# Moving the large SBUF tiles to multiples of 1 KB, and swapping two first loads

## The chip, the cores and the metric

The kernel runs on one core of a Trainium2 chip. The metric is device time in microseconds, the median over runs of the same program.

## What is computed

One layer of a hybrid decoder on 256 tokens of width 2048, all in float32. Cut to what matters here:

```python
h = rmsnorm(x, ln_g)
proj = h @ w_in + b_in                      # 2048 -> 18956 columns
# mLSTM branch (6 heads), retention branch (6 heads), both causal over 256 tokens
ml_out  = head_layernorm(mlstm(silu(conv(q, k)), v, i, f)) * sigmoid(o) * silu(z)
rt_out  = head_layernorm(retention(rope(q), rope(k), v)) * silu(z)
# cross-attention (4 heads) into 256 memory tokens
mk, mv  = split(rmsnorm(mem, mem_ln_g) @ w_mem_kv)
xa_out  = softmax(xa_q @ mk.T / 16) @ mv * silu(xa_z)
merged  = g0 * (ml_out @ w_br_ml) + g1 * (rt_out @ w_br_ret) + g2 * (xa_out @ w_br_xa)
y       = rmsnorm(x + merged @ w_out, final_g)
```

## The kernel before, in words

**The products.** Every weight matrix is cut into column chunks, 512 columns wide (the last two of `w_out` 256 wide). A chunk's weights come in slabs `raw` of 128 partitions x 2048 float32, one DMA of 1 MB each on SP's queue, three buffers deep. ScalarE rounds half a slab to fp32r (`wh`, 1024 columns, four buffers) and VectorE writes the rest `raw - wh` (`wl`, four buffers). The activations are split the same way into a high and a low tile. For every block of 128 rows and every half of the tokens `products` then issues three matmuls into one PSUM bank: `wh` with the high activations, `wl` with the high ones, `wh` with the low ones. Below, these three are a **triple**. The activations are the stationary operand (`lhsT`, 128 x 128, 512 B a partition), the weights the moving one (`rhs`, 512 columns, 2 KB a partition):

```python
PE.matmul(ps, lhsT=h, rhs=a, start=kt == 0, stop=False)          # L924: wh, high
PE.matmul(ps, lhsT=h, rhs=b, start=False, stop=False)            # L925: wl, high
PE.matmul(ps, lhsT=l, rhs=a, start=False, stop=kt == nk - 1)     # L926: wh, low
```

**Where the stationary operand lies.** Four pairs of buffers serve as high and low activations, one pair at a time: `mgd` and `oT1` for the memory tokens (`w_mem_kv`); `aTh` and `aTl` for x (`w_in`); parts of `oT1` and `oT2` for a branch's output (`w_br_*`); and `aTh` and `aTl` once more for the merged branches (`w_out`). The buffer number is left out in the profile, so `oT1` and `oT2` read as `oT`. While the memory tokens are in work, the slot of `aTl` holds their raw form (`memraw`).

**Order of the work.** All instructions are recorded in the order in which they are to stand (a manual schedule). `split` runs three half slabs ahead of `products`; between two half slabs one step of a background job (attention, mLSTM and retention cores, convolution, rotary, transposes) is put in. TensorE is one stream of both.

**Addresses.** The pool gives every tag its place in a partition in the order in which `til` first names it, at the next multiple of 32 B, behind 1 KB that is reserved. Small tiles therefore shift everything that is named after them.

**The start.** ScalarE's queue issues the first piece of memory tokens (`memraw[:, 0, :]`, 128 KB) and then `memG`, the norm weights of the memory tokens (8 KB); SP's queue issues the first slab's pieces and the other memory tokens. The first work of ScalarE, `split_act` (L269), multiplies the one by the other and so needs both.

Of the kernel before, what the change touches and what calls it, by code (L numbers as in the profile page):

```python
# [9 lines left out]
F32R = mybir.dt.float32r  # L10
I32 = mybir.dt.int32
# [5 lines left out]
P = 128  # L17
D = 2048
T = 256
NKT = D // P  # L20
NML = 6
# [7 lines left out]
CST_W = NKT + 48 + 12 * 3 + 1 + 64 + P + P  # L29
# [121 lines left out]
def body(ctx, tc, A, out):  # L151
    nc = tc.nc
    V, S, G, PE = nc.vector, nc.scalar, nc.gpsimd, nc.tensor
# [6 lines left out]
    def til(tag, shape, dt=F32, bufs=1):  # L160
        names[tag] = names.get(tag, 0) + 1
        return sb.tile(shape, dt, tag=tag, name=f"{tag}_{names[tag]}", bufs=bufs)

    def bank(tag="bg", bufs=4):
        names[tag] = names.get(tag, 0) + 1
        return pp.tile([P, 512], F32, tag=tag, name=f"{tag}_{names[tag]}", bufs=bufs)
# [4 lines left out]
    def f32(ap):  # L171
        return ap.bitcast(F32)
# [19 lines left out]
    n = _ROWS["w_mem_kv"] // 512  # L192
# [3 lines left out]
    halves = {}  # L196


    memG = til("memG", [P, NKT])
    memraw = til("aTl", [P, NKT, T])  # L200
    S.dma_start(memraw[:, 0, :], A["memT"][:, 0, :])
    S.dma_start(memG, A["mem_ln_g"])
    ones = til("ones", [P, P])
    G.memset(ones, 1.0)
    nhalf = til("nhalf", [P, 4])
    G.memset(nhalf, -0.5)
    S.copy(til("warm", [P, 1]), ones[:, 0:1])
    wps = bank()
    for _ in range(NWARM):
        PE.matmul(wps[:, :P], lhsT=ones, rhs=ones, start=True, stop=True)  # L210
# [36 lines left out]
    for si in range(NRAW):  # L247
        dma(si)

    cst = til("cst", [P, CST_W])  # L250
    off = [0]

    def part(w):
        off[0] += w
        return cst[:, off[0] - w:off[0]]
# [1 line left out]
    xG, convw, convb = part(NKT), part(48).rearrange("p (b k) -> p b k", k=4), part(12)  # L257
    hg = {"ml_hnorm_g": part(12), "ret_hnorm_g": part(12)}
    bif, freq, ident, mask = part(1), part(64), part(P), part(P)
    posi = til("posi", [P, 2], I32)  # L260
    dret = [None]

    aTh = til("aTh", [P, NKT, T], F32R)
    aTl = til("aTl", [P, NKT, T], F32R)
    ssq = {n: til("ss_" + n, [P, 2]) for n in ("mem", "x")}
    rms = {n: til("r_" + n, [P, 2]) for n in ("mem", "x")}

    def split_act(h, l, src, g):
        S.activation(h, src, AF.Copy, bias=0.0, scale=g)  # L269
# [57 lines left out]
                split_act(aTh[:, kt, :], aTl[:, kt, :], raw[:, k * T:(k + 1) * T], xG[:, kt:kt + 1])  # L327


    cosT = til("cosT", [P, 2, 64])  # L330
    sinT = til("sinT", [P, 2, 64])
    inv2pi = _inv2pi_parts()

    def trig_job():
# [46 lines left out]
        yield  # L381


    MT = til("MT", [P, T], F32R)
    sel = til("sel", [P, NML], F32R)
    cT = til("cT", [P, 2, P])
    enm = til("enm", [P, 2, NML])

    def gate_rows_job(psif):
        rows = iter(range(8))  # L390
# [41 lines left out]
        G.memset(zero, 0.0)  # L432
        G.tensor_copy(MT, zero)
        V.tensor_tensor(sel, ident[:, 0:6], ident[:, 32:38], op=ALU.add)
# [6 lines left out]
        V.scalar_tensor_tensor(RT[64:70], b, -1.0, M, op0=ALU.mult, op1=ALU.subtract)  # L441
        V.tensor_copy(MT[:6], M)
        V.tensor_tensor(MT[32:38], M, f32(MT[:6]), op=ALU.subtract)
        yield
# [161 lines left out]
    def ml_core(h):  # L606
        p, hh = divmod(h, 2)

        mb = bank()
        PE.matmul(mb[:, :T], lhsT=sel[:, h:h + 1].to_broadcast([P, P]), rhs=MT, start=True, stop=True)  # L610
        dm = til("core", [P, 512], bufs=4)
# [67 lines left out]
    gs = {}  # L679
    merged = [None]  # L680
    bigy = {}
    st_out = til("ssy", [P, 2, 5])
    sumsq = til("sumsq", [P, 2])

    def silu_into(dst, ps, bias, r, extra=None):
        zu = stage()
# [276 lines left out]
def _inv2pi_parts():  # L963

    from fractions import Fraction
    pi = Fraction(314159265358979323846264338327950288419716939937510582097494459230781640628620899,
                  10 ** 80)
    x = 1 / (2 * pi)
    parts, shift = [], 14
    for i in range(5):  # L970
        sc = 2 ** shift
        c = Fraction(int(x * sc), sc)
        parts.append(float(c))
        x -= c
        shift += 12
    return parts
# [53 lines left out]
def _build(host):  # L1030
    import concourse.bacc as bacc
    nc = bacc.Bacc("TRN2", target_bir_lowering=False, num_devices=1, dynamic_dma_scratch_size=1024)
    A, arrays = {}, {}
    for n, v in host.items():
        arrays[f"in_{n}_dram"] = v
        A[n] = nc.dram_tensor(f"in_{n}_dram", v.shape, mybir.dt.from_np(v.dtype), kind="ExternalInput").ap()
    out = nc.dram_tensor("out_0_dram", (1, T, D), F32, kind="ExternalOutput").ap()
    with tile.TileContext(nc) as tc:
        body(tc, A, out[0])
    return nc, arrays  # L1040
# [7 lines left out]
```

## Time and profile before

| | |
|---|---|
| median of 3 runs | 1222.71 us (1222.61 to 1223.24) |
| the profiled execution, its own time | 1222.62 us |
| its span in the trace | 1220.6 us |
| TensorE busy | 1211.6 us (99% of the span) |
| VectorE busy | 759.0 us (62%) |
| ScalarE busy | 585.9 us (48%) |
| TensorE's granted clock, share of full speed | 0.999 |

The span is what the trace covers; the 2.0 us between it and the execution's own time lie around it. A busy share is an average over the whole span.

### The profile page before, as it was taken

What the parts mean: (1) busy time and instruction counts of PE and PEld (TensorE: products, weight loads), DVE (VectorE), ACT (ScalarE), POOL (GpSimd) and SP (SyncE); (2) the same over time, 40 slices, a digit from 0 to 9 for tenths busy, and PEclk for the clock granted to TensorE, in tenths of its full rate; (3) what the DMA queues carried; (4) which work ended last, traced back from release to release, by engine and by line L of the source; (5) the groups of instructions that cost most, each with busy time, mean ns of one, the idle gap of its engine ahead of it and who ended that gap; (6) DMA issues with size and microseconds to landing.
All of it is one profiled execution on the core that took longest, in us unless ns stands there. A gap on an engine that the chain in (4) does not pass through costs nothing.

```text
span 1220.6 us, 14366 instructions
## 1 busy us (share of the span) xinstructions
PE 1211.6 (99%) x5490; PEld 1004.2 (82%) x5490; DVE 759.0 (62%) x994; ACT 585.9 (48%) x705; POOL 143.0 (12%) x164
## 2 busy tenths in 40 slices
PE   9999999999999999999999999999999999999997
PEld 7888888888888888888888888888888888888887
DVE  6564576565557576776775555657767665567554
ACT  6665454445434554554555443344444444444443
POOL 0006404400000130130120102101010000000001
PEclk9999999999999999999999999999999999999999
DMA  9876656565556547657547555575657665567752
GB/s 370 317 288 237 238 194 214 200 212 188 205 206 233 200 173 262 215 178 274 202 171 281 194 193 201 196 250 173 237 211 242 232 217 214 186 240 257 290 187 90
DMA packets 61413, 270.65 MB, mean 222 GB/s; under 512 B 7072, under 2 KB 22304, under 8 KB 33312
## 3 DMA queue, kind: packets, MB, share of 16 engines
q1 hardware_dynamic: 56592, 258.06, 59.7%
q10 hardware_dynamic: 4752, 11.68, 2.6%
q8 instruction: 43, 0.70, 0.2%
q14 instruction: 26, 0.21, 0.0%
HBM read 256.60 MB, written 13.11 MB: 221 GB/s over the span
## 4 chain that ended last, share of the span: by engine, by line
PE 98%; DMA 0%; issue 0%; DVE 0%; SPq 0%; ACT 0%; POOLq 0%; POOL 0%; DVEq 0%; ACTq 0%
PE d L925 32%; PE d L924 32%; PE d L926 31%; PE bg L517 1%; PE bg L492 1%; DMA raw<-in_w_dram 0%; PE bg L602 0%; PE bg L604 0%; PE bg L603 0%; PE bg L664 0%; PE bg L622 0%; PE bg L880 0%; PE bg L879 0%; PE bg L508 0%; PE bg L665 0%
## 5 line engine op out<-in xcount | busy, mean ns | idle before, releaser
L274 DVE TENSOR_TENSOR wl<-raw,wh 128x1024 fp32r<-128x1024 f32 (+1 forms) x432 | 528.1, 1229 | 385.9 <-ACT wh L273 385.3
L273 ACT CAST wh<-raw 128x1024 fp32r<-128x1024 f32 (+1 forms) x432 | 443.6, 1033 | 477.4 <-PE d L926 421.7
L924 PE MATMUL d<-wh,aTh 128*128 128x512 f32 (+1 forms) x1344 | 522.4, 389 | 0.0
L925 PE MATMUL d<-wl,aTh 128*128 128x512 f32 (+1 forms) x1344 | 521.3, 388 | 0.0
L926 PE MATMUL d<-wh,aTl 128*128 128x512 f32 (+1 forms) x1344 | 516.8, 385 | 0.0
L924 PEld LDWEIGHTS d<-wh,aTh 128*128 128x128 f32 x1344 | 252.4, 188 | 54.0
L926 PEld LDWEIGHTS d<-wh,aTl 128*128 128x128 f32 x1344 | 252.3, 188 | 53.1
L925 PEld LDWEIGHTS d<-wl,aTh 128*128 128x128 f32 x1344 | 252.7, 188 | 48.4
L926 PE MATMUL d<-wh,oT 128*128 128x512 f32 x384 | 149.4, 389 | 0.0
L924 PE MATMUL d<-wh,oT 128*128 128x512 f32 x256 | 99.6, 389 | 0.0
L925 PE MATMUL d<-wl,oT 128*128 128x512 f32 x256 | 99.6, 389 | 0.0
L926 PEld LDWEIGHTS d<-wh,oT 128*128 128x128 f32 x384 | 72.1, 188 | 15.0
L925 PEld LDWEIGHTS d<-wl,oT 128*128 128x128 f32 x256 | 48.1, 188 | 10.0
L924 PEld LDWEIGHTS d<-wh,oT 128*128 128x128 f32 x256 | 48.1, 188 | 10.0
L689 POOL TENSOR_TENSOR gz<-gz,st 128x512 f32<-128x512 f32 x16 | 21.5, 1357 | 259.9 <-ACT gz L688 259.9
L924 PE MATMUL d<-wh,mgd 128*128 128x512 f32 x128 | 50.1, 392 | 0.2 <-ACT wh L273 0.2
L925 PE MATMUL d<-wl,mgd 128*128 128x512 f32 x128 | 50.0, 391 | 0.3 <-DVE wl L274 0.2
L831 POOL TENSOR_TENSOR oT<-oT,oT 128x512 f32<-128x512 f32 (+1 forms) x8 | 9.2, 1159 | 214.6 <-ACT st L829 214.6
L558 POOL TENSOR_TENSOR k<-k,gs 128x1024 f32<-128x1024 f32 x3 | 7.4, 2472 | 212.7 <-ACT k L556 212.7
L459 DVE SCALAR_TENSOR_TENSOR st<-d,r_x,bias 128x512 f32<-128x512 f32 x44 | 31.4, 744 | 0.0
L924 PEld LDWEIGHTS d<-wh,mgd 128*128 128x128 f32 x128 | 24.1, 188 | 5.8 <-ACT wh L273 0.8
L925 PEld LDWEIGHTS d<-wl,mgd 128*128 128x128 f32 x128 | 24.0, 188 | 5.8 <-DVE wl L274 1.0
(192 smaller groups left out, 626.5 us busy)
## 6 DMA issues: line engine op xcount, KB each, us to landing
raw<-in_w_dram SPq DMA_DIRECT2D x209, 1024.0 KB, 4.8
bias<-in_bias_dram SPq DMA_DIRECT2D x37, 256.0 KB, 5.2
td<-tx SPq DMA_DIRECT2D x52, 128.0 KB, 2.8
ty<-td ACTq DMA_DIRECT2D x13, 512.0 KB, 5.0
td<-tx SPq DMA_DIRECT2D x64, 64.0 KB, 3.2
ty<-td ACTq DMA_DIRECT2D x16, 256.0 KB, 5.6
oT<-in_x_dram SPq DMA_DIRECT2D x3, 1024.0 KB, 7.1
raw<-in_w_dram SPq DMA_DIRECT2D x5, 512.0 KB, 6.8
```

The costliest lines, as they stand in the source:

```text
L273: S.copy(wh, raw)
L274: V.tensor_tensor(wl, raw, f32(wh), op=ALU.subtract)
L459: V.scalar_tensor_tensor(dst, ps, r, bias, op0=ALU.mult, op1=ALU.add)
L492: PE.matmul(ps[:, tb * T:(tb + 1) * T], lhsT=qT[:, 2 * hh + db, tb * P:(tb + 1) * P], rhs=kT[:, 2 * hh + db, :], start=db == 0, stop=db == 1)
L517: PE.matmul(ps[:, tb * T:(tb + 1) * T], lhsT=pT[:, c:c + P], rhs=v[:, mb, hh * T:(hh + 1) * T], start=mb == 0, stop=mb == 1)
L558: G.tensor_tensor(qf, qf, yf, op=ALU.mult)
L689: G.tensor_tensor(dst, dst, zu, op=ALU.mult)
L831: G.tensor_tensor(y, y, g[:, c0:c0 + W], op=ALU.mult)
L924: PE.matmul(ps, lhsT=h, rhs=a, start=kt == 0, stop=False)
L925: PE.matmul(ps, lhsT=h, rhs=b, start=False, stop=False)
L926: PE.matmul(ps, lhsT=l, rhs=a, start=False, stop=kt == nk - 1)
```

## The change

Two things are done. First, the small tiles (norm weights, constants, tables, sums) are all named at the top of `body`, followed by an unused tile of 256 B, `fill`; the first large tile, `aTl`, and all that follow then begin at 7168 B. No tile changes its size and no large tile its neighbours, but `aTh` no longer has the small tiles around it. The places before and now:

```
tile (B a partition)     before: address, mod 1024     now: address, mod 1024
aTl    (16384)              1216   192                    7168     0
mgd    (16384)             18176   768                   23552     0
oT1    (16384)             34560   768                   39936     0
gs     (12288)             50944   768                   56320     0
oT2    (8192)              63232   768                   68608     0
raw    (3 x 8192)          71424   768                   76800     0
aTh    (16384)             97728   448                  101376     0
wh     (4 x 4096)         117504   768                  117760     0
wl     (4 x 4096)         133888   768                  134144     0
st     (4 x 2048)         150272   768                  150528     0
k      (2 x 4096)         158464   768                  158720     0
v      (2 x 4096)         183040   768 (2nd: 800)       183296     0 (2nd: 32)
q      (4160)             195424   864                  195680    96
core   (4 x 2048)         209888   992                  210144   224
```

Second, ScalarE's queue issues `memG` first and the first piece of memory tokens after it. The core of the diff:

```diff
     memG = til("memG", [P, NKT])
+    nhalf = til("nhalf", [P, 4])
+    warm = til("warm", [P, 1])
+    ones = til("ones", [P, P])
+    cst = til("cst", [P, CST_W])
...
+    MT = til("MT", [P, T], F32R)
+    cT = til("cT", [P, 2, P])
+    til("fill", [P, 64])
     memraw = til("aTl", [P, NKT, T])
+    S.dma_start(memG, A["mem_ln_g"])
     S.dma_start(memraw[:, 0, :], A["memT"][:, 0, :])
-    S.dma_start(memG, A["mem_ln_g"])
-    ones = til("ones", [P, P])
     G.memset(ones, 1.0)
-    nhalf = til("nhalf", [P, 4])
     G.memset(nhalf, -0.5)
-    S.copy(til("warm", [P, 1]), ones[:, 0:1])
+    S.copy(warm, ones[:, 0:1])
```

On ScalarE's queue the head of the program stood so before (a name's number is the buffer's):

```order
L201 DMA aTl_66<-in_memT_dram 128x256
L202 DMA memG_65<-in_mem_ln_g_dram 128x16
L207 ACT_TABLE_LOAD
L207 COPY warm_73<-ones_69 128x1
L269 ACTIVATE mgd_86<-aTl_66,memG_65 128x256
L273 CAST wh_119<-raw_90 128x512
```

and stands so now:

```order
L217 DMA memG_65<-in_mem_ln_g_dram 128x16
L218 DMA aTl_84<-in_memT_dram 128x256
L221 ACT_TABLE_LOAD
L221 COPY warm_67<-ones_68 128x1
L279 ACTIVATE mgd_101<-aTl_84,memG_65 128x256
L283 CAST wh_120<-raw_105 128x512
```

The two loads have changed places; no other instruction of any engine has moved, which the triples of a `w_in` chunk on TensorE show for the middle of the program, before:

```order
L924 MATMUL d_29_4758<-wh_4865,aTh_105 128x512
L925 MATMUL d_29_4758<-wl_4866,aTh_105 128x512
L926 MATMUL d_29_4758<-wh_4865,aTl_106 128x512
L924 MATMUL d_29_4759<-wh_4865,aTh_105 128x512
L925 MATMUL d_29_4759<-wl_4866,aTh_105 128x512
```

and now, at the same place:

```order
L926 MATMUL d_29_4759<-wh_4866,aTh_118 128x512
L927 MATMUL d_29_4759<-wl_4867,aTh_118 128x512
L928 MATMUL d_29_4759<-wh_4866,aTl_119 128x512
L926 MATMUL d_29_4760<-wh_4866,aTh_118 128x512
L927 MATMUL d_29_4760<-wl_4867,aTh_118 128x512
```

Only the line numbers and the numbers of the buffers differ: lines of `products` are two higher, and the operands lie elsewhere.

## Rows read from the trace of the kernel before

**Rows 1.** The page: busy time, and the chain that ended last.

```profile
PE 1211.6 (99%) x5490; PEld 1004.2 (82%) x5490; DVE 759.0 (62%) x994; ACT 585.9 (48%) x705; POOL 143.0 (12%) x164
...
PE 98%; DMA 0%; issue 0%; DVE 0%; SPq 0%; ACT 0%; POOLq 0%; POOL 0%; DVEq 0%; ACTq 0%
```

**Rows 2.** Waits of TensorE: us in total, times, longest.

```profile
PE bg L210 <- POOL nhalf L206: 1.0, 1, 1.0
PE d L924 <- ACT wh L273: 0.2, 1, 0.2
PE d L925 <- DVE wl L274: 0.2, 1, 0.2
```

**Rows 3.** Groups by form, whole span: busy us, mean ns of one.

```profile
L924 PE MATMUL d<-wh,aTh 128*128 128x512 f32 x1280 | 504.5, 394 | 0.0
...
L924 PE MATMUL d<-wh,oT 128*128 128x512 f32 x256 | 99.6, 389 | 0.0
L924 PE MATMUL d<-wh,mgd 128*128 128x512 f32 x128 | 50.1, 392 | 0.2 <-ACT wh L273 0.2
...
L926 PE MATMUL d<-wh,aTl 128*128 128x256 f32 x64 | 17.9, 280 | 0.0
```

**Rows 4.** Timeline of TensorE: first and last high product of 450 to 480.

```profile
450.27 0.39 PE L924 MATMUL d<-wh,aTh 128*128 128x512 f32 x1
...
479.79 0.39 PE L924 MATMUL d<-wh,aTh 128*128 128x512 f32 x1
```

**Rows 5.** Windows of line 924 alone: length, busy (count), weight loads, clock, DMA, GB/s.

```profile
450.00:480.00 30.00, 17.06 (x44) 8.26 (x44) 1.00 0.77 270
720.00:750.00 30.00, 17.20 (x45) 8.26 (x44) 1.00 0.53 180
...
30.00:60.00 30.00, 17.12 (x44) 8.31 (x45) 1.00 0.87 320
...
141.80:150.20 8.40, 4.77 (x12) 2.24 (x12) 1.00 0.55 203
```

**Rows 6.** Timeline of TensorE: first and last high product of 720 to 750.

```profile
719.96 0.39 PE L924 MATMUL d<-wh,oT 128*128 128x512 f32 x1
...
749.88 0.39 PE L924 MATMUL d<-wh,oT 128*128 128x512 f32 x1
```

**Rows 7.** Timeline of TensorE: first and last high product of 30 to 60.

```profile
30.25 0.39 PE L924 MATMUL d<-wh,mgd 128*128 128x512 f32 x1
...
59.49 0.39 PE L924 MATMUL d<-wh,mgd 128*128 128x512 f32 x1
```

**Rows 8.** Timeline of TensorE in a `w_out` chunk.

```profile
1184.87 0.39 PE L924 MATMUL d<-wh,aTh 128*128 128x512 f32 x1
...
1186.93 0.39 PE L924 MATMUL d<-wh,aTh 128*128 128x512 f32 x1
```

**Rows 9.** Timeline of TensorE after the gate rows, to the next background matmuls.

```profile
141.89 0.40 PE L924 MATMUL d<-wh,aTh 128*128 128x512 f32 x1
...
149.59 0.40 PE L924 MATMUL d<-wh,aTh 128*128 128x512 f32 x1
...
150.29 1.89 PE L492 MATMUL bg<-k,q 128*128 128x256 f32 x8
```

**Rows 10.** Chain that ended last, to 20 us: start, us, what.

```profile
2.57 5.94 DMA raw<-in_w_dram
8.52 0.02 issue
8.54 0.63 ACT wh L273
```

**Rows 11.** Timeline of ScalarE at the start, with idle time before.

```profile
4.79 0.51 ACT L269 ACTIVATE mgd<-aTl,memG 128x256 fp32r<-128x256 f32 x1 [1.66 <-DMA memG<-in_mem_ln_g_dram]
...
8.54 0.62 ACT L273 CAST wh<-raw 128x512 fp32r<-128x512 f32 x1 [1.05 <-DMA raw<-in_w_dram]
```

**Rows 12.** DMA issues of the first 2 us: KB each, us to landing.

```profile
aTl<-in_memT_dram ACTq DMA_DIRECT2D x1, 128.0 KB, 3.6
aTl<-in_memT_dram SPq DMA_DIRECT2D x1, 128.0 KB, 3.4
memG<-in_mem_ln_g_dram ACTq DMA_DIRECT2D x1, 8.0 KB, 3.5
```

**Rows 13.** Waits of the whole span: ScalarE for TensorE.

```profile
ACT wh L273 <- PE d L926: 421.7, 277, 3.4
```

**Rows 14.** Timeline at 654 us: a split on VectorE, and the product that uses it.

```profile
654.31 1.23 DVE L274 TENSOR_TENSOR wl<-raw,wh 128x1024 fp32r<-128x1024 f32 x1 [0.20 <-ACT wh L273]
...
655.87 0.39 PE L925 MATMUL d<-wl,aTh 128*128 128x512 f32 x1
```

More of the change, by code (lines that the diff above doesn't have):

```diff
@@ L199, in body @@
     memG = til("memG", [P, NKT])
+    nhalf = til("nhalf", [P, 4])
+    warm = til("warm", [P, 1])
+    ones = til("ones", [P, P])
+    cst = til("cst", [P, CST_W])
+    posi = til("posi", [P, 2], I32)
+    ssq = {n: til("ss_" + n, [P, 2]) for n in ("mem", "x")}
+    rms = {n: til("r_" + n, [P, 2]) for n in ("mem", "x")}
+    cosT, sinT = (til(n, [P, 2, 64]) for n in ("cosT", "sinT"))
+    sel = til("sel", [P, NML], F32R)
+    enm = til("enm", [P, 2, NML])
+    st_out = til("ssy", [P, 2, 5])
+    sumsq = til("sumsq", [P, 2])
+    MT = til("MT", [P, T], F32R)
+    cT = til("cT", [P, 2, P])
+    til("fill", [P, 64])
     memraw = til("aTl", [P, NKT, T])
+    S.dma_start(memG, A["mem_ln_g"])
     S.dma_start(memraw[:, 0, :], A["memT"][:, 0, :])
-    S.dma_start(memG, A["mem_ln_g"])
-    ones = til("ones", [P, P])
     G.memset(ones, 1.0)
-    nhalf = til("nhalf", [P, 4])
     G.memset(nhalf, -0.5)
-    S.copy(til("warm", [P, 1]), ones[:, 0:1])
+    S.copy(warm, ones[:, 0:1])
     wps = bank()
@@ L248, in body @@
         dma(si)
-    cst = til("cst", [P, CST_W])
     off = [0]
@@ L259, in body @@
     bif, freq, ident, mask = part(1), part(64), part(P), part(P)
-    posi = til("posi", [P, 2], I32)
     dret = [None]
@@ L264, in body @@
     aTl = til("aTl", [P, NKT, T], F32R)
-    ssq = {n: til("ss_" + n, [P, 2]) for n in ("mem", "x")}
-    rms = {n: til("r_" + n, [P, 2]) for n in ("mem", "x")}
     def split_act(h, l, src, g):
@@ L327, in split_aux @@
                 split_act(aTh[:, kt, :], aTl[:, kt, :], raw[:, k * T:(k + 1) * T], xG[:, kt:kt + 1])
-    cosT = til("cosT", [P, 2, 64])
-    sinT = til("sinT", [P, 2, 64])
     inv2pi = _inv2pi_parts()
@@ L381, in trig_job @@
         yield
[L384 to L387, printed above, removed]
     def gate_rows_job(psif):
@@ L681, in body @@
     bigy = {}
-    st_out = til("ssy", [P, 2, 5])
-    sumsq = til("sumsq", [P, 2])
     def silu_into(dst, ps, bias, r, extra=None):
```

## The prediction

> **What bounds the kernel now.** I read the page first. TensorE is busy for 1211.6 of 1220.6 us, and the chain that ended last runs through TensorE for 98% of the span [rows 1]. The waits of TensorE confirm it: one of 1.0 us before the warm-up and two of 0.2 us near the start, nothing later [rows 2]. Behind them the other engines wait for TensorE and not the reverse: ScalarE stood 421.7 us in all until a product had freed a `wh` buffer [rows 13]. So an edit changes the time only if it changes how densely matmuls follow each other, or when their stream begins.
>
> A busy engine need not be at its best, so the next view is the spacing of the matmuls, by stationary operand. The change moves operands, and the spacing is the only thing in the trace that could feel an address. A duration in the profile spans several matmuls in the pipeline (392 or 389 ns, with starts some 228 ns apart), so I go from start to start. In an undisturbed `w_in` stretch the high product of line 924 starts at 450.27 us and the last one at 479.79 us [rows 4]; 44 of them stand there [rows 5], so 43 triples took 29.52 us: 686.5 ns each, 228.8 ns a matmul. In a branch projection, 45 starts from 719.96 to 749.88 us [rows 5, 6] give 44 triples in 29.92 us: 680.0 ns. In the memory stage, 44 starts from 30.25 to 59.49 us [rows 5, 7] give 43 triples in 29.24 us: 680.0 ns again. All three ran at a granted clock of 1.00, the 2.4 GHz level [rows 5].
>
> The three stretches do the same arithmetic with the same shapes and with the same `wh` and `wl` slots as moving operand. What differs is the stationary operand's place: 768 mod 1024 for `mgd`, `oT1` and `oT2`, which is also that of `wh` and `wl`; 448 and 192 for `aTh` and `aTl`. The stage is not the cause: in `w_out`, with other data and other background work but once more in the `aTh` and `aTl` slots, three triples take 1186.93 - 1184.87 = 2.06 us, 687 ns [rows 8]. Nor is traffic: the DMA engines were busy for a share of 0.77 in the slow stretch, but for 0.87 in the memory stage, which is at 680 [rows 5]. And `mgd` with `oT1`, two separate tiles, is as fast as `oT1` with `oT2`. I conclude that a stationary operand at 64 mod 128 (as 448 and 192 both are) costs TensorE some 6.5 ns a triple, or that one at another remainder than the moving operand does; the trace can't tell these apart.
>
> **The change, part by part.**
>
> *Large tiles to 1 KB.* The order of instructions stays, so the same 1,280 triples of 512 columns run from `aTh` and `aTl` [rows 3]. Both slots go to 0 mod 1024, and `wh` and `wl` too; their blocks lie 512 B apart, so stationary and moving operand then stand to each other as `mgd` and `wh` do now, and the remainder mod 128 is 0. Under either reading they take the 680.0 ns of the other stages: 1,280 x 6.5 ns = **8.3 us** less.
>
> Some stretches are slower than 686.5. After the gate rows twelve starts run from 141.89 to 149.59 us [rows 5, 9]: eleven triples in 7.70 us, 700 ns each. Such stretches come back a few times and are short. If they also fall to 680, this one gives another 12 x 13.5 ns = 0.16 us. The mean duration of a high product from `aTh`, 394 ns against 389 from `oT` [rows 3], also holds matmuls that queue behind background ones, and an address won't free those. I bound this term by 0 and by six stretches of the size shown, 1.0 us, and take **0.6 us**, since the memory and branch stages show a high product at the same 389 whatever runs beside them.
>
> The last two chunks have 64 triples of 256 columns [rows 3], for which no operand at another place is on record. I bound them by 0 and by the same 6.5 ns, 0.4 us, and take **0.2 us**, the middle.
>
> The triples of `mgd` and `oT` (128 and 256) [rows 3] move from 768 to 0 with `wh` and `wl` together; nothing relative changes, and I take 0. The background tiles (`k`, `q`, `v`, `core`) all move by 256 B together and stay off 1 KB where they were off it: 0. VectorE, ScalarE and the DMAs also read and write at other places, but work ahead of TensorE [rows 13], so a change there is hidden. That cover is thinnest where I found a split on VectorE ending at 655.54 us for a product that began at 655.87 us [rows 14], a lead of 0.33 us. TensorE 1% faster over the some 30 us before would use up 0.3 us of it. If that lead goes under, the wait is a few tenths of a us, at that place; I allow 0.3 us as a bound and take 0.
>
> *The two loads of ScalarE's queue.* Before, the first ACTIVATE starts at 4.79 us, when `memG` lands, having waited 1.66 us [rows 11]. It took 3.5 us to land, and a piece of memory tokens 3.6 us on the same queue and 3.4 us on SP's [rows 12]. A swap therefore exchanges which of the two lands second; the second is issued at the same time and needs 3.4 to 3.6 us in either case, so the first ACTIVATE moves by -0.1 to +0.1 us, or later if 128 KB behind the other loads take longer. But what ends last at the start is neither. The chain runs through the first slab's third piece, ordered at some 2.1 us, on its way until 8.52 us and rounded at 8.54 us [rows 10]; ScalarE stood idle for 1.05 us before that [rows 11]. So an earlier `memG` gains nothing, and tokens that come up to 1.05 us later cost nothing. Bounds: 0.3 us either way, for the slab's piece that shares the engines with the swapped load. Value: 0.
>
> **Sum.** 8.3 + 0.6 + 0.2 = 9.1 us. The profiled execution took 1222.62 us, 0.1 us under the median of 1222.71, so from the median the forecast is 1222.7 - 9.1 = **1213.6 us**. Bounds: the gain is at least 8.3 - 0.3 - 0.3 = 7.7 us and at most 8.3 + 1.0 + 0.4 + 0.3 = 10.0 us, which is 1212.7 to 1215.0.
>
> **Rivals.**
>
> *No change.* The 6.5 ns come from something that goes with `aTh` and `aTl` but not with their remainder, say from how far they lie from `wh`, which hardly changes (`aTh` still ends just below `wh`). For it: the three matmuls of a triple aren't slowed alike, which a plain alignment cost would do. Against it: the 16 blocks of `aTh` and the four buffers of `wh` lie at many distances, and 43 triples in a row show one mean. Time: 1222.7 less at most the 0.3 us of the start, 1222.4 to 1223.
>
> By the Trainium skill the address shouldn't count either. TensorE: Matmul & The Clock Gate gives TensorE two independent read ports, one for the moving and one for the stationary operand (Step-by-step: what each phase is for), and a spacing that follows from the column count alone, 512/2.4 + 2.5 = 216 ns (Back-to-back issue gap). By that page the sum would be 0. The trace doesn't agree: neither 226.7 nor 228.8 ns is 216, and the spacing depends on the slot.
>
> *Slower: a common start at 0 collides.* If reads of both operands that begin at 0 mod 1024 hamper each other more than those at 768, every triple of 512 columns could run at the 700 ns that this kernel knows [rows 9]: 1,280 x 13.5 ns + 384 x 20 ns = 25 us, 1248 us. Against it: at 768 they share a remainder already and are the fastest. It decides from the first stretch on: a spacing above 680 ns in the memory stage would say so; over 2.4 us are lost once the 1,664 triples average 1.5 ns more than now.
>
> *A larger gain.* 226.7 ns is still 13 ns above 512/2.4 = 213.3. If 0 mod 1024 is better than 768 as 768 is better than 448, by 6.5 ns on each of 1,664 triples, another 10.8 us go: 1203 us. No row shows an operand of this size at 0, so it stays a small chance.
>
> **Chances.** The forecast 0.80, no change 0.11, slower 0.04, the larger gain 0.05. What a measurement of this kernel can tell from no change is some 0.2%, 2.4 us. So: faster 0.85, same 0.11, slower 0.04. The range must hold 8 in 10 and so may leave out the rivals, but holds the forecast's own bounds with 0.6 us for the spread of runs, and at the slow end a gain that is only three quarters of the main term, as it is if one of the two slots keeps a part: 1211.5 to 1216.0 us.
>
> **What would show it.** In the trace after: triples of `aTh` at 680 ns between 450 and 480 us (or still 686.5: no change), those of `mgd` still at 680; no 700 ns stretch after the gate rows; the first continuous product still at some 10 us, behind the same piece of the slab; TensorE's waits still only at the start. I am wrong if the spacing is a matter of place and not of alignment, or if 0 isn't as good as 768.

## The result, and the profile after

The changed kernel takes 1216.19 us, the median of 6 runs (1215.39 to 1218.67), against 1222.74 us for the kernel before in 6 runs beside it: a ratio of 0.9947, 95% interval 0.9934 to 0.996. It is faster by 6.5 us, where 9.1 were forecast, and 0.2 us above the range.

The triples are where the forecast saw them. The timeline of TensorE after, at the place of [rows 4]:

```profile
450.50 0.39 PE L926 MATMUL d<-wh,aTh 128*128 128x512 f32 x1
...
479.74 0.39 PE L926 MATMUL d<-wh,aTh 128*128 128x512 f32 x1
```

29.24 us are 43 triples of 680.0 ns (the window below counts 45 products, of which one had begun at 449.82 us), where there were 686.5. The windows of the high product after, against [rows 5]:

```profile
450.00:480.00 30.00, 17.20 (x45) 8.26 (x44) 1.00 0.76 269
720.00:750.00 30.00, 17.12 (x44) 8.29 (x45) 1.00 0.55 191
30.00:60.00 30.00, 17.12 (x44) 8.32 (x45) 1.00 0.83 313
```

All three stages now hold the same number of triples but for the edges. The chain is still TensorE's, with 98%.

Two things went the other way. The first is at the end. Groups by form of the 256-column products, after (before: 280 ns, [rows 3]), and the timeline in their midst:

```profile
L928 PE MATMUL d<-wh,aTl 128*128 128x256 f32 x64 | 18.1, 283 | 0.0
```

```profile
1200.80 0.28 PE L926 MATMUL d<-wh,aTh 128*128 128x256 f32 x1
...
1202.96 0.28 PE L926 MATMUL d<-wh,aTh 128*128 128x256 f32 x1
```

Six triples in 2.16 us are 360 ns each. Before, six took 2.12 us, 353.3 ns each:

```profile
1204.15 0.28 PE L924 MATMUL d<-wh,aTh 128*128 128x256 f32 x1
...
1206.27 0.28 PE L924 MATMUL d<-wh,aTh 128*128 128x256 f32 x1
```

The second is the start, in this one execution. Windows of the first 16 us after: length, busy (count) of TensorE, its weight loads, VectorE, ScalarE, GpSimd, then granted clock, DMA share, GB/s:

```profile
0.00:4.00 4.00, 3.02 (x15) 3.02 (x16) 0.00 (x0) 1.48 (x2) 0.43 (x6) 1.00 0.50 147
4.00:8.00 4.00, 2.44 (x12) 1.74 (x11) 1.57 (x3) 1.43 (x3) 0.00 (x0) 0.91 0.92 302
8.00:12.00 4.00, 3.64 (x8) 2.11 (x7) 2.44 (x5) 3.03 (x6) 0.00 (x0) 0.50 1.01 405
12.00:16.00 4.00, 4.00 (x15) 3.18 (x14) 3.38 (x5) 2.98 (x5) 0.00 (x0) 0.74 0.96 363
```

The granted clock fell to 0.50, the 1.2 GHz level, for the stretch from 8 to 12 us and parts of its neighbours. Ahead of that TensorE had been idle: the timeline shows the last warm-up matmul ending at 4.83 us and the first product after a wait of 1.32 us, and the waits of TensorE have a row that [rows 2] lacks:

```profile
6.15 0.49 PE L926 MATMUL d<-wh,mgd 128*128 128x512 f32 x1 [1.32 <-ACT wh L283]
```

```profile
PE d L926 <- ACT wh L283: 1.7, 2, 1.3
```

The first high product from `aTh` came at 97.6 us in place of 94.2, 3.4 us late, while from there to the last one the program was 7.3 us shorter. The tile view of `aTh`, before and after (min/median/max, first and last start):

```profile
L924 PE MATMUL d<-wh,aTh x1344: 279/392/584, 94.2 to 1212.6; 128*128 128x512 f32 x183, 128*128 128x256 f32 x9
```

```profile
L926 PE MATMUL d<-wh,aTh x1344: 278/389/586, 97.6 to 1208.7; 128*128 128x512 f32 x183, 128*128 128x256 f32 x9
```

This profiled execution is the one of 1218.67 us; the other five, with a mean clock of 0.999, took 1215.39 to 1216.61.

### The profile page after: what moved, and what is told of

It reads as the page before. It is cut to its first block, busy times and chain, and to the rows that moved or that the text cites. A ratio compares the mean times of both kernels' runs of the same rounds, so it can differ in the third digit from the quotient of the medians.

```text
span 1216.7 us, 14366 instructions
## 1 busy us (share of the span) xinstructions
PE 1206.4 (99%) x5490; PEld 1005.2 (83%) x5490; DVE 759.4 (62%) x994; ACT 587.2 (48%) x705; POOL 143.0 (12%) x164
## 4 chain that ended last, share of the span: by engine, by line
PE 98%; DMA 1%; issue 0%; DVE 0%; SPq 0%; ACT 0%; POOLq 0%; POOL 0%; DVEq 0%; ACTq 0%
PE d L926 32%; PE d L927 32%; PE d L928 32%; PE bg L496 1%; PE bg L521 1%; DMA raw<-in_w_dram 1%; PE bg L606 0%; PE bg L608 0%; PE bg L607 0%; PE bg L626 0%; PE bg L668 0%; PE bg L882 0%; PE bg L881 0%; PE bg L512 0%; PE bg L627 0%
```

## The experiments

Theory A, formed after the result, had the swap of the two loads, which makes the first product later, to blame for what was missing. On the places there were two readings to tell apart, the place itself or the distance of the operands.

**New places, old order of loads.**

```diff
-    S.dma_start(memG, A["mem_ln_g"])
     S.dma_start(memraw[:, 0, :], A["memT"][:, 0, :])
+    S.dma_start(memG, A["mem_ln_g"])
```

> Theory A (the swap of the two loads costs at the start what is missing): with the large tiles at multiples of 1 KB and the old order of loads, the first product of the memory stage starts at 5.9 us again, the granted clock stays at 1.00 from there on, and the time is 1222.7 - 7.3 = 1215.4 us with a spread of runs under 1 us. Rival B (the new places of the tiles delay the start): the first product still starts at 6.1 us or later, and the runs still lie between 1215.4 and 1218.7 us, with a median of some 1216.2 us. In both, triples from aTh and aTl take 680 ns.

Measured: 1215.69 us (1215.12 to 1216.44), ratio 0.9941 (0.9928 to 0.9953); first product at 5.99 us; triples at 680 ns.

**Old places, new order of loads** (the kernel before with the two lines exchanged).

> Theory A: with the old places and the swapped loads the kernel is slower than before by 0.3 to 3.4 us, different from run to run, with a median of some 1223.5 us; the first product starts at 6.1 us or later. Rival B: 1222.7 us, first product at 5.9 us. Triples from aTh and aTl take 686.7 ns in both.

Measured: 1223.59 us in 11 runs (1222.63 to 1224.22) against 1222.93, ratio 1.0005 (0.9996 to 1.0014): no difference that can be told, though the first product came at 6.32 us. The mean clock lay between 0.997 and 0.999.

**The changed kernel with more warm-up**, `NWARM = 16` for 10.

> The changed kernel with 16 warm-up matmuls in place of 10, which fill TensorE's idle time from 4.8 us to the first product at 6.1 us. Theory A with idle TensorE as the reason for the fall of the granted clock: the clock no longer falls in any run (mean 0.999), and the median is some 1215.5 us. Rival C (the fall has nothing to do with that idle time, only with the later waits for the slab): the clock falls as often as in the changed kernel, median 1216.2 us.

Measured: 1215.61 us (1215.38 to 1215.66), the narrowest of all.

**The changed kernel once more.**

> The changed kernel once more, as a control beside the three others: 1215.4 to 1218.7 us, median 1216.2 us, with a granted clock of 0.995 in the longest runs and 0.999 in the shorter ones, if theory A is right that the loss at the start differs from run to run.

Measured: 1215.82 us (1215.56 to 1216.61), ratio 0.9943 (0.993 to 0.9955), with a mean clock of 0.998 or 0.999 in each run. Windows of its start, first product after 0.54 us of idle time:

```profile
4.00:8.00 4.00, 3.23 (x14) 2.46 (x14) 2.35 (x5) 2.35 (x5) 0.00 (x0) 1.00 0.93 318
8.00:12.00 4.00, 3.81 (x17) 2.84 (x16) 2.69 (x5) 3.28 (x5) 0.00 (x0) 1.00 1.02 416
```

So theory A falls as an account of what was missing: with the new places the swap made 0.13 us of difference (1215.82 against 1215.69 us), which the spread of the runs covers. It isn't shown that the swap is free. With the old places the median rose by 0.66 us, to where theory A had put it; the interval of the ratio still holds 1, so a few tenths of a us are neither shown nor excluded. A mean clock of 0.995, the fall, came once in 11 runs of the changed kernel and in none of the 15 with more warm-up, these and those below: too rare to say that the warm-up cures it.

The mean clock also misses shorter losses. In the trace of the old places with the new order, with a mean of 0.999, the first products stood 0.43 us apart, as in the low stretch of the trace after, where later ones stand 0.23 us apart (the windows of this trace give 1.00 there, so the level is read from the spacing alone):

```profile
8.07 0.63 PE L924 MATMUL d<-wh,mgd 128*128 128x512 f32 x1
...
9.35 0.63 PE L924 MATMUL d<-wh,mgd 128*128 128x512 f32 x1
```

There the first high product from `aTh` came at 95.4 us in place of 94.2. Of the ten traces of the layer's kernel, the three that show this spacing are the three in which TensorE stood idle longest before its first product: 0.60 (the worse distance, below), 0.71 (here) and 1.32 us (the trace after). The three traces with more warm-up, without such idle time, don't show it. That agrees with the second half of theory A, that idle TensorE costs clock, but one or two traces of each kernel don't prove it.

**Placements alone.** A kernel of matmuls on constants, with the operands of a triple at chosen addresses:

```python
x = hi[:, h // 4 + c:h // 4 + c + 128]; y = lo[:, l // 4 + c:l // 4 + c + 128]
a = wh[:, ra // 4 + (k % 2) * 512:][:, :w]; b = wl[:, rb // 4 + (k % 2) * 512:][:, :w]
PE.matmul(d[tb][:, :w], lhsT=x, rhs=a, ...)
PE.matmul(d[tb][:, :w], lhsT=x, rhs=b, ...)
PE.matmul(d[tb][:, :w], lhsT=y, rhs=a, ...)
```

> Only matmuls, on constants; nothing of the layer is computed, no loads, other engines idle. 38 placements of the high and low stationary operand and of wh and wl, each 24 triples of 512 and 24 of 256 columns, back to back. If the place alone sets the spacing, 448/192 against 768 takes 686.7 ns a triple here too, and 353 ns at 256 columns, and 0 against 0 takes 680 and 360 ns. Theory P (place of the stationary operand mod 128 counts): all operands at 64 take 686.7 ns. Theory R (only the distance between stationary and moving operand counts): all at 64 take 680 ns, and 0 against wh at 64 differs from it. Rival M (it takes the traffic of other engines): every placement takes 680 ns.

The timeline, high product of the second and the last of 24 triples, in four placements: all at 0; `hi` at 448 and `lo` at 192 against 768; all at 64; `hi` and `lo` at 64 against 0.

```profile
39.32 0.39 PE L186 MATMUL db<-wh,hi 128*128 128x512 f32 x1
...
54.28 0.39 PE L186 MATMUL db<-wh,hi 128*128 128x512 f32 x1
...
91.06 0.40 PE L186 MATMUL db<-wh,hi 128*128 128x512 f32 x1
...
106.18 0.39 PE L186 MATMUL db<-wh,hi 128*128 128x512 f32 x1
...
168.66 0.40 PE L186 MATMUL db<-wh,hi 128*128 128x512 f32 x1
...
183.63 0.39 PE L186 MATMUL db<-wh,hi 128*128 128x512 f32 x1
...
376.88 0.40 PE L186 MATMUL db<-wh,hi 128*128 128x512 f32 x1
...
392.28 0.40 PE L186 MATMUL db<-wh,hi 128*128 128x512 f32 x1
```

22 triples each: 680.0, 687, 680 and 700 ns. With no load and no other engine at work, the places of before give the spacing of before, so rival M falls; and all operands at 64 are as good as all at 0, so theory P falls. From the starts between the fifth triple and the last of each placement:

```
hi and lo, in B behind wh and wl    512 columns    256 columns    (ns a triple)
  0, 256, 512, 768                    680.0          360.0
 64, 320                              699.9, 700.2   340.0
128, 384, 640, 896                    697.1 to 700.2 356.1 to 356.3
192, 448, 960                         686.7          353.3 to 353.4
all four at 32, 64, 128 or 768        680.0          360.0
448/192 against 768, as before        686.6          353.4
```

In steps of 64 B, what counts is the distance between stationary and moving operand mod 256, not the place, and the best distance at 512 columns, 0, is the worst at 256. The rule isn't exact: at 128 the triples differ by 3 ns, and with `wh` and `wl` moved by 128 B in place of `hi` and `lo` they took 697.0 ns, but 360.0 at 256 columns. For finer steps it fails: three placements at 240 mod 256, in these runs and the next, gave 680.0, 684.8 and 694.8 ns.

**More placements.**

> Only matmuls of 512 columns again, nothing of the layer is computed: 78 placements, with the high and the low stationary operand and wl each at 0, 64, 128 or 192 B from wh, mod 256, and some 16 B steps. If 680 ns is the least that this stream can take, none goes below it. If a distance exists at which the reads get out of each other's way, as 64 B does at 256 columns (340 in place of 360 ns), some placement takes less than 675 ns.

Of 78 none went below 680.0 ns. With only `lo` 64 B off it was 693.3, with only `wl` 64 B off 696.0, so the places of all three operands count. For these steps of 64 B and some of 16, there is no more to gain at 512 columns.

**All large tiles at 64 mod 1024.**

```diff
-    til("fill", [P, 64])
+    til("fill", [P, 80])
```

> The changed kernel with 64 B more of fill, so that all large tiles lie at 64 mod 1024, none at a multiple of 128 B. Theory R (distance between stationary and moving operand, mod 256): triples still take 680 ns and the time is that of the changed kernel, 1215.5 to 1216.5 us. Theory P (the place itself, mod 128 or 1024): 686.7 ns or more in every stage, 1222 us or more.

Measured: 1215.75 us (1215.15 to 1216.04), ratio 0.9941 (0.9923 to 0.9958): theory R, in the kernel itself. The timeline:

```profile
450.19 0.39 PE L926 MATMUL d<-wh,aTh 128*128 128x512 f32 x1
...
479.43 0.39 PE L926 MATMUL d<-wh,aTh 128*128 128x512 f32 x1
```

43 triples in 29.24 us. The multiples of 1 KB are not needed.

**A worse distance**: `aTh` and `aTl` 64 B off, by small tiles ahead of and behind them.

```diff
-    til("fill", [P, 64])
+    til("fill", [P, 16])
     memraw = til("aTl", [P, NKT, T])
...
+    til("fillb", [P, 48])
     memTh = til("mgd", [P, NKT, T], F32R)
...
+    til("fillc", [P, 16])
     aTh = til("aTh", [P, NKT, T], F32R)
+    til("filld", [P, 48])
```

> The changed kernel with aTh and aTl moved to 64 mod 256, 64 B from wh and wl in distance; all other large tiles stay at multiples of 256 B. If the table of distances measured on matmuls alone carries over to the kernel, triples of 512 columns from these two tiles take 700 ns and those of 256 columns 340 ns, the others 680 ns: 1215.8 + 1,280 x 20 ns - 64 x 20 ns = 1240 us, slower than the kernel before by 17 us. If the traffic of the other engines sets another pattern, the 512-column triples lie elsewhere between 680 and 710 ns.

Measured: 1239.45 us (1238.33 to 1239.56), ratio 1.0134 (1.012 to 1.0148). The timeline in a `w_in` stretch and in the last chunk:

```profile
450.46 0.39 PE L929 MATMUL d<-wh,aTh 128*128 128x512 f32 x1
...
479.86 0.39 PE L929 MATMUL d<-wh,aTh 128*128 128x512 f32 x1
```

```profile
1222.07 0.28 PE L929 MATMUL d<-wh,aTh 128*128 128x256 f32 x1
...
1223.77 0.28 PE L929 MATMUL d<-wh,aTh 128*128 128x256 f32 x1
```

42 triples in 29.40 us are 700 ns, five in 1.70 us 340 ns. 64 B cost the kernel 24 us, and the table told it to within 0.6 us. That it came so close is in part luck: against the trace of the control, the triples of 512 columns cost 24.0 us more and not 25.6, those of 256 columns 1.2 less, and all else 1.3 more.

**More warm-up with either order of loads**, side by side.

> New places, old order of the two loads, 16 warm-up matmuls: if the swap costs time at the start, this beats the swapped kernel with 16 warm-up matmuls by 0.1 to 0.7 us; if it is free, the two agree within 0.3 us. 1215.3 us.

> New places, swapped loads, 16 warm-up matmuls, beside the run with the old order: 1215.6 us, spread under 0.5 us, granted clock 0.999 in every run.

Measured: 1215.44 us (1215.37 to 1215.78) with the old order and 1215.60 us (1215.38 to 1216.33) with the new one: no difference that can be told. The forecast for the second, a spread under 0.5 us and a clock of 0.999 in every run, was missed: the spread was 0.95 us and the clock 0.998, so the narrow spread of the first five runs with more warm-up was luck. The first is the lowest median of all kernels here, but only 0.4 us under the control of the changed one, whose runs it overlaps.

## Why the prediction was wrong

**Right: the bound, the mechanism and the main term.** TensorE's spacing depends on where the operands lie; every stage now runs at 680 ns, and `aTh` and `aTl` gave 6.67 ns on each undisturbed triple (686.67 to 680.0, on matmuls alone too). The rival of no change falls, and with it what the Trainium skill would have led to: TensorE: Matmul & The Clock Gate (Back-to-back issue gap) gives the spacing by the column count alone, 216 ns at 512 columns for a single matmul and some 131 ns for a sustained stream of weight loads and matmuls. The trace doesn't agree with either: the best is 226.7 ns, and one shape took 680 to 707 ns a triple by the places of its operands. The rivals of a collision at 0 and of a larger gain fall too: 0 behaves like 768, and nothing was found below 680.0.

**Wrong: the terms beside the main one, two of them in sign.** The sum took 0.6 us of gain from disturbed stretches and 0.2 from the triples of 256 columns; the runs showed a loss of 0.8 and of 0.4 us in their place. The account, from starts in the trace of the kernel before and of the control run, the changed kernel once more (span 1213.5 us), whose clock did not fall:

```
                                               before    control   change   forecast
1,280 triples of 512 columns from aTh, aTl      883.1     875.4     -7.7      -8.9
  if each were 6.67 ns shorter                                      -8.5      -8.3
  triples behind and after background work                          +0.8      -0.6
63 spacings of 256-column triples                22.3      22.7     +0.4      -0.2
all else, the start included                    315.2     315.4     +0.2       0
span                                           1220.6    1213.5     -7.1      -9.1
```

*The term for disturbed stretches* (0.6 us gained, bounds 0 and 1.0) had the wrong sign. The 700 ns stretch of [rows 9] did shrink, to triples of 698 and 690 ns and then 680. But behind other background matmuls the stream now needs longer to settle: in the control run 111 triples lie between 683 and 712 ns, before 68 between 690 and 703, against a steady spacing of 680 and 686.7. Timeline of the control run behind a background matmul of the mLSTM core:

```profile
519.44 0.38 PE L627 MATMUL bg<-k 128*128 128x128 f32 x2
519.58 0.47 PE L926 MATMUL d<-wh,aTh 128*128 128x512 f32 x1
...
520.35 0.40 PE L926 MATMUL d<-wh,aTh 128*128 128x512 f32 x1
...
521.04 0.39 PE L926 MATMUL d<-wh,aTh 128*128 128x512 f32 x1
...
521.73 0.39 PE L926 MATMUL d<-wh,aTh 128*128 128x512 f32 x1
```

After the first triple, which also waits for the background matmul, come 690 ns and 690 ns by these rows (696 and 685 to the nanosecond; before, at the same place, 689 and 687). Of the 0.8 us, 0.2 lie in the 46 triples right behind background work and some 0.4 in those after them.

The last 0.2 us are one wait, at the very place where the prediction saw the thinnest cover [rows 14]. It had allowed for up to 0.3 us there and taken 0. In the control run the weight load of a product waits for VectorE's split, and the triple that began at 651.59 us took 872 ns:

```profile
651.90 0.19 PEld L927 LDWEIGHTS d<-wl,aTh 128*128 128x128 f32 x1 [0.34 <-DVE wl L284]
```

In the two traces of old places no such triple is found; in the trace after it took 822 ns. So TensorE's waits were not only at the start, which the prediction had named as a sign.

The step failed because I took the memory and branch stages as proof that all falls to 680, but a look at what stands ahead of each product shows that 46 products from `aTh` follow a background matmul, one from `mgd` and none from `oT`. The mean of `mgd` was also 392 ns and not 389 [rows 3]. And the trace before held only 0.5 us above the steady spacing in the triples after the first behind background work, less than the 0.6 us that I took and half of the bound.

Why the stream settles more slowly was not tested, but the run with all large tiles at 64 mod 1024 shows a part of it, since there the small tiles alone kept their places. Behind a matmul of `MT` and `sel`, two small tiles, two triples took 1.41 us in the control run:

```profile
513.32 0.40 PE L926 MATMUL d<-wh,aTh 128*128 128x512 f32 x1
...
514.73 0.40 PE L926 MATMUL d<-wh,aTh 128*128 128x512 f32 x1
```

and 1.36 us, the steady spacing, in that run:

```profile
514.23 0.39 PE L926 MATMUL d<-wh,aTh 128*128 128x512 f32 x1
...
515.59 0.39 PE L926 MATMUL d<-wh,aTh 128*128 128x512 f32 x1
```

Behind background matmuls of large tiles alone (`k`; `k` and `q`; `v` and `core`) the two traces lose the same within 2 ns each. By these two traces the place of the background's operands against the stream's counts as well; by what rule stays open.

*The term for 256 columns* (0.2 us gained, bounds 0 and 0.4) had the wrong sign too: I carried the 6.5 ns over from 512 columns. By the table above, the distance that is best there costs 7 ns here, and the kernel shows it, 360 for 353.3 ns.

*The start* (0, bounds 0.3) was right in value for the control run, whose first high product from `aTh` came at 94.3 us, but the bounds did not hold the one execution in which the clock fell, 3.4 us. It lifts the median of 6 runs little; without it the other five have 1215.93. In the control the gain is 1222.93 - 1215.82 = 7.1 us: the time is inside the range, the gain under the 7.7 us that the prediction called the least. What made the clock fall there is not shown. The first product came at 6.15 us in both executions, so its load was not later. But the warm-up matmuls were over at 4.83 us and in the control at 5.61 us, so TensorE stood idle for 1.32 us in place of 0.54. The rows of the trace after and of the control:

```profile
0.98 3.85 PE L224 MATMUL bg<-ones 128*128 128x128 f32 x20 [0.98 <-POOL nhalf L220]
```

```profile
0.98 4.63 PE L224 MATMUL bg<-ones 128*128 128x128 f32 x20 [0.98 <-POOL nhalf L220]
```

In the trace after, the last seven of them start 112 ns apart and not 213, as at the higher of the two clock levels; why the clock rose sooner there is open.

*The range* was also cut closer than its reason: three quarters of the main term are 6.2 us, which by itself is 1216.5 us and not 1216.0.

**Left open by the prediction, and settled:** place or distance. It is the distance, in steps of 64 B mod 256.

## What to carry to other kernels

Where TensorE is the bound, compare start-to-start spacings of one shape between stages: a difference of 1% with the clock at full speed can be a matter of where the two operands lie, and a few bytes of small tiles between large ones decide it. Place stationary and moving operand so that their distance is the best for the width that most matmuls have, and measure it for each width, since 512 and 256 columns want different ones. Don't carry a gain over to another shape, or to the triples behind other work, without a row of it. And where a faster stream comes close to a split that feeds it, count that wait in.

## What the runs showed of the hardware

For fp32r matmuls with a new 128 x 128 stationary operand each, 512 columns took 226.7 ns at best (680.0 a triple) at a granted clock of 1.00, and up to 235.5 ns (706.6 a triple) with other distances between the operands; 256 columns took 113.3 to 120 ns. It happens with the other engines idle and no loads on the way. What in TensorE does it was not tried.
